# A two-number reordering in a hybrid-attention block: query norms two filler steps later, pair splits two attention steps later

## The chip, the cores and the metric

The kernel runs on one core of one Trainium2 chip. The metric is the device time of one execution in microseconds (us); lower is better. TensorE (PE in the profile) does the matrix products, and PEld is its weight load; VectorE is DVE, ScalarE is ACT, GpSimd is POOL; SP only starts transfers.

## The reference

One transformer block in float32, for 512 tokens of width 1024:

```
h = h + 0.5 * swiglu(rmsnorm(h, ffn1_norm), ffn1_w_gu, ffn1_w_down)
u = rmsnorm(h, mix_norm)
qa, ka, va, qb, kb, vb, qi, ki, wi, g = split(u @ w_in)
qa, ka, qb, kb = each head's rmsnorm, with its gain
out_a = dsa_attention(qa, ka, va, qi, ki, wi, bias_dsa)   # 8 heads, top-128 keys per query
out_b = moba_attention(qb, kb, vb, bias_moba)             # 8 heads, blocks of 256 keys
mixed = g_a * (out_a @ w_branch_dsa) + g_b * (out_b @ w_branch_moba)
h = h + mixed @ w_out
h = h + 0.5 * swiglu(rmsnorm(h, ffn2_norm), ffn2_w_gu, ffn2_w_down)
```

The heads are 64 wide, so two heads (a pair) fill 128 partitions. The hidden width of both feed-forward parts is 2816.

## The kernel before, in words

**Products.** Every float32 operand is split into a rounded high part and a low remainder, and each product is three matmuls (`mm3`, L126 to L128). A weight comes in by a transfer to `raw`, ACT writes `whi` (L111), POOL writes `wlo` in four pieces (L117). An activation is split by `split`: ACT writes the high part (L153), DVE the low one (L154).

**Stages.** First feed-forward part, then the mixer, then the second feed-forward part. The mixer runs the MoBA attention, the selection of keys, the MoBA branch, then the DSA attention and its branch. Each attention is a generator of 32 steps, for 8 heads times 4 tiles of 128 queries. Step `i` issues the logits of tile `i + 2` (PE L619 and L620 into one of two `s` banks; DVE L628 adds bias and takes the minimum; ACT L75 exponentiates), then `turn(i)` transposes the probabilities (PE L659, one to four 128-column transposes into a `pt` bank, which ACT L669 copies as the high part and DVE L670 as the low part), then, where `i % 4 == 1`, `values` of the head before: PE L680 and L681 into the one `o` bank, ACT L686, DVE L687 into `os`. After the second head of a pair POOL divides by the softmax sums (L690), and the pair's output is split (L153, L154). Its consumer, the branch product, runs only after all heads.

**What fills the gaps.** Between the steps `weave` takes units of the next projections as filler; every filler step is one `mm3` or a pair of them and calls `tick()`. Work that must not stand right behind its producer is queued with `later(n, fn)` and issued at the n-th tick from there. A query projection (`q_post`) squares its result (ACT L430 into a `tmp` buffer), and `later(LAG_Q, norm)` issues four tiny matmuls that sum the squares (L441, into a `pt` bank), DVE L444 that empties the bank, and a chain of small operations (ACT L75, DVE L447 to L451). A key projection does the like with `LAG` (L475, L476, L478, L479, L485, L486). Value projections end in ACT L500 and DVE L501, which empty an `mm` bank.

**Order and buffers.** The order on PE is the order in which the program is written; on the other engines a scheduler sets it. PSUM banks: `mm` 3, `s` 2, `pt` 2, `o` 1. A new `pt` tile takes whichever of the two banks comes free first, and its first matmul waits for the last reader of what the bank held.

Of the kernel before, what the change touches and what calls it, by code (L numbers as in the profile page):

```python
# [31 lines left out]

PIN, EVERY = (0, 20, 28, 31), 2

LAG, LAG_Q = 11, 4

SPIN, HURRY = 10, 200

# [7 lines left out]
def f32(ap):  # L46
    return ap.bitcast(F32)
# [3 lines left out]
def block_kernel(ctx, tc, x, gains, wgu1, wd1, w_in, w_v, wb_a, wb_b, w_out, wgu2, wd2, rel_bias, onehot, out):  # L51
# [30 lines left out]
    def log_exp(out, src, fn, **k):  # L82
        table_op("natural_log_exp_and_others", out, src, fn, **k)
# [3 lines left out]
    def T(tag, bufs, shape=(P, S), dt=F32, p=sb):  # L87
        uid[0] += 1
        return p.tile(list(shape), dt, tag=tag, name=f"{tag}{uid[0]}", bufs=bufs)

    def tmp(dt=F32):
        return T("tmp", TMPS, (P, S), dt)
# [4 lines left out]
    def sps():  # L97
        return T("s", 2, p=ps)

    def tps():  # L100
        return T("pt", 2, p=ps)
# [46 lines left out]
    def pair_a():  # L148
        return T("a", 16, (P, S), F32R), T("a", 16, (P, S), F32R)

    def split(dst, src):
        hi, lo = dst
        nc.scalar.activation(hi, src, AF.Copy)  # L153
        nc.vector.tensor_sub(lo, src, f32(hi))  # L154
        return dst
# [206 lines left out]
    def bias_tile(hd):  # L362
        t = T("bias", 2)
        f0 = fd[hd:hd + 1, 0:S]
        nc.sync.dma_start(t, bass.AP(f0.tensor, f0.offset, [[1, P], [1, S]]))
        return t
# [214 lines left out]
    def attention(br, pairs, outs, extra):  # L581

        sel = br == 0
        bias, prob, tms, osum, tot, inv_s = {}, {}, {}, {}, {}, {}

        def table(hd):
            if hd < 8:
                bias[hd] = bias_tile(br * 8 + hd)

        def rows(qt):  # L590
            return T(f"l{qt}", 2 if qt == 0 else 1, (P, P * (qt + 1)))

        def addend(i):

            if i < 32:
                hd, qt = divmod(i, 4)
                W = P * (qt + 1)
                inv = pairs[hd // 2][0][2][:, 2 * qt + hd % 2:2 * qt + hd % 2 + 1]
                tms[i] = rows(qt)
                b = bias[hd][:, S - W:S]  # L600
                if sel and qt:
                    nc.vector.scalar_tensor_tensor(tms[i], b, inv, work[:, WOFF[qt]:WOFF[qt] + W],
                                                   op0=ALU.mult, op1=ALU.add)
                else:
                    nc.gpsimd.tensor_scalar(tms[i], b, inv, 1.0, op0=ALU.mult, op1=ALU.mult)

        def logits(i):
            if i >= 32:
                return
            hd, qt = divmod(i, 4)  # L610
            if qt == 1:
                table(hd + 1)
            e = hd % 2
            (q, f, _), (k, kl), _ = pairs[hd // 2]
            W = P * (qt + 1)
            N = max(W, 256)
            p = sps()
            qb = q[:, e, qt * P:(qt + 1) * P]
            nc.tensor.matmul(p[:, 0:N], qb, k[:, e, 0:N], start=True, stop=False)  # L619
            nc.tensor.matmul(p[:, 0:N], qb, kl[:, e, 0:N], start=False, stop=True)  # L620
            addend(i + 1)
            pe = tms.pop(i)
            st = T("st", 8, (P, 4))
            if i % 8 == 0:
                tot[hd // 2] = T("tot", 2, (P, 8))
            s1 = tot[hd // 2][:, i % 8:i % 8 + 1]
            with tc.high_priority(HURRY):
                sums[i] = nc.vector.tensor_tensor_reduce(  # L628
                    out=pe, in0=p[:, 0:W], in1=pe, scale=f[:, 2 * qt + e:2 * qt + e + 1], scalar=3e38, op0=ALU.add, op1=ALU.min, accum_out=st[:, 0:1])
                log_exp(pe, pe, AF.Exp, bias=st[:, 0:1], scale=-1.0, accum_out=s1)  # L630
            prob[i] = pe

        def norms(pr, p):

            row = rows_d[turns[1] % 2]
            turns[1] += 1
            nc.vector.reciprocal(r1[:, 0:8], tot.pop(pr))
            nc.tensor.transpose(p, r1, ident)
            o = p[0:8, P - 1:P]
            rw = T("rw", 2, (8, P))  # L640
            nc.scalar.activation(rw, bass.AP(o.tensor, o.offset, [list(o.ap[0]), [-1, P]]), AF.Copy)
            nc.sync.dma_start(row, rw)
            rb = inv_s[pr] = T("rb", 2)
            for e in range(2):
                a = row[4 * e:4 * e + 1, :]
                nc.sync.dma_start(rb[HALF[e], :], bass.AP(a.tensor, a.offset, [[0, DH], [1, S]]))

        def turn(i):
            hd = i // 4
            if i % 4 == 0:  # L650
                return
            pp = tps()
            c, parts = 0, []
            for j in (i - 1, i) if i % 4 == 1 else (i,):
                qt = j % 4
                pe = prob.pop(j)
                parts.append((qt, pp[:, c:c + (qt + 1) * P].rearrange("p (k c) -> p k c", c=P)))
                for kt in range(qt + 1):
                    nc.tensor.transpose(pp[:, c:c + P], pe[:, kt * P:(kt + 1) * P], ident)  # L659
                    c += P  # L660
            if i % 8 == 6:
                norms(i // 8, pp[:, c:c + P])
            pth, ptl = pts[hd % 2]
            for qt, src in parts:
                def dst(a):
                    o = a[:, qt * P + P - 1:qt * P + P]
                    return bass.AP(o.tensor, o.offset, [list(o.ap[0]), [384, qt + 1], [-1, P]])

                nc.scalar.activation(dst(pth), src, AF.Copy)  # L669
                nc.vector.tensor_sub(dst(ptl), src, dst(f32(pth)))  # L670

        def values(hd):
            e = hd % 2
            v = pairs[hd // 2][2][0]
            pth, ptl = pts[hd % 2]
            po = T("o", 1, p=ps)
            for kt in range(NQ):
                q0 = min(kt, 2) * P
                c = 384 * kt + q0
                nc.tensor.matmul(po[:, q0:S], v[:, kt, e, :], pth[:, c:c + S - q0], start=kt == 0, stop=False)  # L680
                nc.tensor.matmul(po[:, q0:S], v[:, kt, e, :], ptl[:, c:c + S - q0], start=False, stop=kt == NQ - 1)  # L681
            if e == 0:
                osum[0] = T("os", 1)
            ot = tmp()
            with tc.high_priority(HURRY):
                nc.scalar.activation(ot[0:DH, :], po[DH:P, :], AF.Copy)  # L686
                nc.vector.tensor_add(osum[0][e * DH:(e + 1) * DH, :], po[0:DH, :], ot[0:DH, :])  # L687
            if e == 1:
                eng = nc.vector if sel and hd == 7 else nc.gpsimd
                eng.tensor_mul(osum[0], osum[0], inv_s.pop(hd // 2))  # L690
                outs.append(split(pair_a(), osum[0]))

        table(0)
        addend(0)
        logits(0)
        yield 2
        logits(1)
        yield 1
        for i in range(32):
            logits(i + 2)  # L700
            yield 1
            turn(i)
            yield 1
            if i % 4 == 1 and i > 4:
                values(i // 4 - 1)
            if extra and i % EVERY == 0:
                extra.pop(0)()
            yield 1
        yield 3
        values(7)  # L710

    def weave(att, filler, ahead):
        for _ in range(ahead):
            next(filler, None)
        for n in att:
            for _ in range(n):
                next(filler, None)
# [65 lines left out]
    for u, post in ((U_KI, ki_post), (U_QI, qi_post), (U_QI + 1, qi_post)):  # L783
# [5 lines left out]
    fill = chain(qk(1, 1) + qk(1, 2) + [vv(1, 1)] + qk(1, 3) + [gate(KD + c, gates) for c in range(GATES_B)]  # L789
                 + qk(0, 0) + [vv(0, 0)])  # L790
    weave(attention(1, moba, ob, extra), fill, AHEAD_B)
    run(fill)
    for qt in range(1, NQ):
        topk(qt)
    mixb = [T("a", 16) for _ in range(KD)]
    for c in range(KD):
# [3 lines left out]
        run(branch(wb_b, c, ob, lambda p: nc.vector.tensor_mul(mixb[c], p, g1)))  # L800
    fill = chain(qk(0, 1) + qk(0, 2) + [vv(0, 1)] + qk(0, 3) + [gate(c, gates) for c in range(GATES)])
    weave(attention(0, dsa, oa, []), fill, AHEAD_A)
    run(fill)
    flush()
# [105 lines left out]
```

## Time and profile before

| what | value |
|---|---|
| time of three runs | 1139.1, 1139.22, 1141.05 us (median 1139.22) |
| the profiled execution | 1139.47 us, span of its instructions 1137.7 us |
| granted TensorE clock | 1.000 over the whole span |
| busy: PE, DVE, ACT, POOL | 1130.0, 646.2, 469.9, 549.3 us |
| busy from 482 to 527 us: PE, DVE | 43.84, 43.71 of 45 us |

The profile is of one execution, 0.25 us above the median. The span leaves 1.77 us of it outside. Times in the rows are counted from the start of the span; "busy" of PE counts overlapping matmuls once. A name such as `pt` or `mm` stands for all tiles of that kind.

### The profile page before, as it was taken

To read this page: it belongs to the slowest core of one execution; us is meant where nothing else is said; L and a number is where in the kernel's file an instruction comes from. 1 tells how busy PE (TensorE), PEld (TensorE's weight loads), DVE (VectorE), ACT (ScalarE), POOL (GpSimd) and SP (SyncE) were. 2 spreads that over 40 slices of the span, in tenths; PEclk is the share of its full clock that TensorE was granted. 3 is DMA by queue.
4 is the path that set the end of the run, shared out by engine and by line. 5 is a ranking of instruction groups with operands and counts; after the bars stand their busy time and mean duration, and the time that the engine had idled before them with its cause. 6 is when DMAs were issued, how large, how long until landed. Compare 5 with 4: busy or idle time off the path is not lost.

```text
span 1137.7 us, 14242 instructions
## 1 busy us (share of the span) xinstructions
PE 1130.0 (99%) x5364; PEld 947.0 (83%) x5364; DVE 646.2 (57%) x971; ACT 469.9 (41%) x770; POOL 549.3 (48%) x435
## 2 busy tenths in 40 slices
PE   9999999999999999999999999999999999999998
PEld 8888888888888888888889888888888888888887
DVE  6853156613557458699958785754663156613641
ACT  6432123312325568768238766444332123212321
POOL 3444444444446574665564551174444444444443
PEclk9999999999999999999999999999999999999999
DMA  7233222322323222321232321422233232322322
GB/s 237 94 118 95 93 97 105 95 93 93 106 71 114 83 101 84 102 75 52 98 131 93 110 67 47 139 93 97 103 98 93 93 105 100 93 93 96 104 70 102
DMA packets 39580, 111.73 MB, mean 98 GB/s; under 512 B 4534, under 2 KB 9048, under 8 KB 39512
## 3 DMA queue, kind: packets, MB, share of 16 engines
q1 hardware_dynamic: 39080, 110.28, 29.4%
q8 instruction: 42, 0.69, 0.2%
q10 hardware_dynamic: 432, 0.55, 0.2%
q14 instruction: 26, 0.21, 0.1%
HBM read 108.64 MB, written 2.17 MB: 97 GB/s over the span
## 4 chain that ended last, share of the span: by engine, by line
PE 92%; DVE 5%; ACT 2%; issue 1%; POOL 1%; POOLq 0%; DVEq 0%
PE mm L126 22%; PE mm L127 22%; PE mm L128 22%; PE s L126 7%; PE s L128 7%; PE s L127 7%; PE pt L659 1%; DVE l L628 1%; PE s L619 1%; PE s L620 1%; DVE work L566 1%; PE o L681 1%; PE o L680 1%; POOL wlo L117 1%; DVE pt L670 0%
## 5 line engine op out<-in xcount | busy, mean ns | idle before, releaser
L117 POOL TENSOR_TENSOR wlo<-raw,whi 128x256 fp32r<-128x256 f32 (+2 forms) x344 | 491.6, 1449 | 528.7 <-ACT whi L111 517.4
L111 ACT ACTIVATE whi<-raw 128x1024 fp32r<-128x1024 f32 (+2 forms) x206 | 203.8, 994 | 509.5 <-PE mm L127 325.8
L126 PE MATMUL mm<-x,whi 128*128 128x512 f32 x630 | 249.6, 396 | 1.1 <-DVE v L501 1.1
L128 PE MATMUL mm<-x,wlo 128*128 128x512 f32 x630 | 245.9, 390 | 0.0
L127 PE MATMUL mm<-x,whi 128*128 128x512 f32 x630 | 245.9, 390 | 0.0
L126 PE MATMUL mm<-a,whi 128*128 128x512 f32 (+1 forms) x462 | 178.5, 386 | 0.0
L127 PE MATMUL mm<-a,whi 128*128 128x512 f32 (+1 forms) x462 | 178.5, 386 | 0.0
L128 PE MATMUL mm<-a,wlo 128*128 128x512 f32 (+1 forms) x462 | 178.4, 386 | 0.0
L128 PEld LDWEIGHTS mm<-x,wlo 128*128 128x128 f32 x630 | 118.2, 188 | 25.3
L126 PEld LDWEIGHTS mm<-x,whi 128*128 128x128 f32 x630 | 118.4, 188 | 22.8 <-DVE v L501 1.6
L127 PEld LDWEIGHTS mm<-x,whi 128*128 128x128 f32 x630 | 118.5, 188 | 21.3 <-DVE x L207 0.4
L126 PE MATMUL s<-x,whi 128*128 128x512 f32 x342 | 133.1, 389 | 0.0
L128 PE MATMUL s<-x,wlo 128*128 128x512 f32 x342 | 133.0, 389 | 0.0
L127 PE MATMUL s<-x,whi 128*128 128x512 f32 x342 | 133.0, 389 | 0.0
L289 DVE SCALAR_TENSOR_TENSOR h<-mm,h 128x512 f32<-128x512 f32 (+1 forms) x49 | 33.3, 681 | 167.6 <-PE mm L128 167.6
L275 DVE TENSOR_TENSOR tmp<-tmp,tmp 128x512 f32<-128x512 f32 x44 | 97.0, 2205 | 30.4 <-ACT tmp L75 30.1
L154 DVE TENSOR_TENSOR a<-tmp,a 128x512 fp32r<-128x512 f32 x49 | 86.4, 1764 | 28.5 <-ACT a L153 28.3
L126 PEld LDWEIGHTS mm<-a,whi 128*128 128x128 f32 x462 | 86.8, 188 | 17.6
L127 PEld LDWEIGHTS mm<-a,whi 128*128 128x128 f32 x462 | 86.8, 188 | 17.6
L128 PEld LDWEIGHTS mm<-a,wlo 128*128 128x128 f32 x462 | 86.8, 188 | 17.6
L128 PEld LDWEIGHTS s<-x,wlo 128*128 128x128 f32 x342 | 64.2, 188 | 13.4
L126 PEld LDWEIGHTS s<-x,whi 128*128 128x128 f32 x342 | 64.2, 188 | 13.3
(196 smaller groups left out, 1361.8 us busy)
## 6 DMA issues: line engine op xcount, KB each, us to landing
raw<-in_ffn_w_gu_dram SPq DMA_DIRECT2D x84, 512.0 KB, 3.5
raw<-in_w_in_dram SPq DMA_DIRECT2D x35, 512.0 KB, 3.5
raw<-in_ffn_w_down_dram SPq DMA_DIRECT2D x32, 512.0 KB, 3.5
raw<-in_ffn_w_down_dram SPq DMA_DIRECT2D x16, 384.0 KB, 3.1
bias<-fd SPq DMA_DIRECT2D x16, 256.0 KB, 3.4
raw<-in_w_v_dram SPq DMA_DIRECT2D x8, 512.0 KB, 3.4
raw<-in_w_out_dram SPq DMA_DIRECT2D x8, 512.0 KB, 3.5
raw<-in_ffn_w_gu_dram SPq DMA_DIRECT2D x16, 128.0 KB, 3.9
```

Of the source, the lines that this page charges most:

```text
L111: nc.scalar.activation(hi, raw, AF.Copy)
L117: eng.tensor_sub(lo[:, b], raw[:, b], f32(hi)[:, b])
L126: nc.tensor.matmul(pt, wh, xh, start=start, stop=False)
L127: nc.tensor.matmul(pt, wh, xl, start=False, stop=False)
L128: nc.tensor.matmul(pt, wl, xh, start=False, stop=stop)
L154: nc.vector.tensor_sub(lo, src, f32(hi))
L275: nc.vector.tensor_mul(g1, g1, s)
L289: nc.vector.scalar_tensor_tensor(h[c][:, b], pd, 0.5, h[c][:, b], op0=ALU.mult, op1=ALU.add)
L566: nc.vector.match_replace(out=acc, in_to_replace=m8, in_values=acc, imm_value=-2e38)
L619: nc.tensor.matmul(p[:, 0:N], qb, k[:, e, 0:N], start=True, stop=False)
L620: nc.tensor.matmul(p[:, 0:N], qb, kl[:, e, 0:N], start=False, stop=True)
L628: sums[i] = nc.vector.tensor_tensor_reduce(out=pe, in0=p[:, 0:W], in1=pe, scale=f[:, 2 * qt + e:2 * qt + e + 1], scalar=3e38, op0=ALU.add, ...
```

## The change

Two edits. `LAG_Q` goes from 4 to 6, so each query projection's four L441 matmuls, and with them the chain behind them, are issued two filler steps later; there are 8 such groups. And a finished pair's split (L153, L154) is no longer issued at the end of `values` but kept in a list, and `drop()` issues it at `i % 4 == 3`, two attention steps later; this holds for three pairs of each attention, while the last pair's is issued at once as before. Every instruction of before is there once; only places differ.

```diff
-LAG, LAG_Q = 11, 4
+LAG, LAG_Q = 11, 6
...
             if e == 1:
                 eng = nc.vector if sel and hd == 7 else nc.gpsimd
                 eng.tensor_mul(osum[0], osum[0], inv_s.pop(hd // 2))
-                outs.append(split(pair_a(), osum[0]))
+                done.append(osum[0])
+
+        done = []
+
+        def drop():
+            while done:
+                outs.append(split(pair_a(), done.pop()))
...
             if i % 4 == 1 and i > 4:
                 values(i // 4 - 1)
+            if i % 4 == 3:
+                drop()
             if extra and i % EVERY == 0:
                 extra.pop(0)()
             yield 1
         yield 3
         values(7)
+        drop()
```

How that moves instructions is shown at three places. The first is PE in the MoBA attention, from 425.7 to 428.5 us of the profile before: `pt_3255` (then `pt_3269`) holds the sums of squares, `pt_3283` the three transposes of a query tile. Before:

```order
L441 MATMUL pt_3255<-bd,tmp_3186 128x2 x4
L126 MATMUL mm_3193<-x_2536,whi_3195 128x512
L127 MATMUL mm_3193<-x_2537,whi_3195 128x512
L128 MATMUL mm_3193<-x_2536,wlo_3196 128x512
L619 MATMUL s_3272<-k_2959,q_2835 128x256
L620 MATMUL s_3272<-low_2642,q_2835 128x256
L126 MATMUL mm_3193<-x_2569,whi_3195 128x512
L127 MATMUL mm_3193<-x_2570,whi_3195 128x512
L128 MATMUL mm_3193<-x_2569,wlo_3196 128x512
L659 MATMUL pt_3283<-ident,l_3167 128x128 x3
```

And now:

```order
L126 MATMUL mm_3193<-x_2536,whi_3195 128x512
L127 MATMUL mm_3193<-x_2537,whi_3195 128x512
L128 MATMUL mm_3193<-x_2536,wlo_3196 128x512
L619 MATMUL s_3258<-k_2959,q_2835 128x256
L620 MATMUL s_3258<-low_2642,q_2835 128x256
L126 MATMUL mm_3193<-x_2569,whi_3195 128x512
L127 MATMUL mm_3193<-x_2570,whi_3195 128x512
L128 MATMUL mm_3193<-x_2569,wlo_3196 128x512
L441 MATMUL pt_3269<-bd,tmp_3186 128x2 x4
L659 MATMUL pt_3283<-ident,l_3167 128x128 x3
```

L441 went from eight matmuls ahead of the transposes to directly ahead of them. The same happens to the group of four L441 at 479.3 us and to that at 615.4 us, which in addition stood ahead of the eight L680 and L681 of `values` and now stands behind them.

The second place is DVE behind the group of 615.4 us, in the DSA attention, from 617.1 to 622.4 us: `pt_5452` is the pair of query tiles transposed before, whose second piece (128x2x128) L670 reads last, and `pt_5466` (then `pt_5500`) the sums of squares. Before:

```order
L444 TENSOR_TENSOR fq_5471<-pt_5466,r2q 128x8
L435 SCALAR_TENSOR_TENSOR q_5384<-mm_5309,gqk,q_5384 64x512
L670 TENSOR_TENSOR pt_2655<-pt_5452,pt_2654 128x128
L229 SCALAR_TENSOR_TENSOR tmp_5438<-mm_5434,tmp_5438 128x512
L687 TENSOR_TENSOR os_5489<-o_5480,tmp_5490 64x512
L628 ISA l_5423,st_5504<-s_5499,l_5423,fq_5264 128x128
L628 ISA st_5504 128x1
L478 SCALAR_TENSOR_TENSOR tmp_5438<-tmp_5438,tmp_5437 128x512
L670 TENSOR_TENSOR pt_2655<-pt_5452,pt_2654 128x2x128
```

And now:

```order
L435 SCALAR_TENSOR_TENSOR q_5384<-mm_5309,gqk,q_5384 64x512
L670 TENSOR_TENSOR pt_2655<-pt_5452,pt_2654 128x128
L229 SCALAR_TENSOR_TENSOR tmp_5438<-mm_5434,tmp_5438 128x512
L687 TENSOR_TENSOR os_5475<-o_5466,tmp_5476 64x512
L628 ISA l_5423,st_5490<-s_5485,l_5423,fq_5270 128x128
L628 ISA st_5490 128x1
L478 SCALAR_TENSOR_TENSOR tmp_5438<-tmp_5438,tmp_5437 128x512
L670 TENSOR_TENSOR pt_2655<-pt_5452,pt_2654 128x2x128
L479 TENSOR_TENSOR tmp_5437<-tmp_5301,tmp_5438 128x512
L444 TENSOR_TENSOR fq_5505<-pt_5500,r2q 128x8
```

L444 moved from eight rows ahead of the second L670 to two rows behind it; the rows between are the same.

The third place is ACT in the DSA attention from 633.7 to 638.2 us, where a pair's split met the value projection; the unsigned rows and the signs give the order before (-) and now (+):

```order
 L500 ACTIVATE v_5550<-mm_5407,r2T 128x2x64
-L153 ACTIVATE a_5653<-os_5489 128x512
+L669 ACTIVATE pt_2652<-pt_5685 128x3x128
 L500 ACTIVATE v_5550<-mm_5560,r2T 128x2x64
-L669 ACTIVATE pt_2652<-pt_5689 128x3x128
+L153 ACTIVATE a_5720<-os_5475 128x512
 L500 ACTIVATE v_5551<-mm_5407,r2T 128x2x64
```

L153 moved behind one L500 and one L669, but still stands ahead of the L500 that is the last to read `mm_5407` on ACT. On DVE its partner L154 moved from ahead of the L628 and L501 of this stretch to behind them.

## Rows read from the trace of the kernel before

**Rows 1.** The page: the span, PE's busy time, DVE and PEclk in 40 slices.

```profile
span 1137.7 us, 14242 instructions
...
PE 1130.0 (99%) x5364; PEld 947.0 (83%) x5364; DVE 646.2 (57%) x971; ACT 469.9 (41%) x770; POOL 549.3 (48%) x435
...
DVE  6853156613557458699958785754663156613641
...
PEclk9999999999999999999999999999999999999999
```

**Rows 2.** Timeline of PE, each late matmul and its predecessor: start, duration, what; [idle, releaser].

```profile
435.16 0.40 PE L127 MATMUL mm<-x,whi 128*128 128x512 f32 x1
435.39 0.39 PE L128 MATMUL mm<-x,wlo 128*128 128x512 f32 x1
436.53 0.50 PE L619 MATMUL s<-k,q 128*128 128x512 f32 x1 [0.75 <-DVE st L628]
...
522.60 0.28 PE L127 MATMUL mm<-wlo,x 128*128 128x256 f32 x1
522.72 0.28 PE L128 MATMUL mm<-whi,x 128*128 128x256 f32 x1
523.51 1.05 PE L441 MATMUL pt<-bd,tmp 128*128 128x2 f32 x8 [0.52 <-ACT tmp L430]
...
525.11 0.28 PE L128 MATMUL mm<-whi,x 128*128 128x256 f32 x1
526.03 0.66 PE L659 MATMUL pt<-ident,l 128*128 128x128 f32 x4 [0.64 <-DVE pt L670]
...
636.87 0.40 PE L128 MATMUL mm<-x,wlo 128*128 128x512 f32 x1
638.41 0.50 PE L126 MATMUL mm<-x,whi 128*128 128x512 f32 x1 [1.14 <-DVE v L501]
```

**Rows 3.** Timeline of PE and DVE around the first place, 426.6 to 430.2 us.

```profile
426.69 0.17 DVE L444 TENSOR_TENSOR fq<-pt,r2q 128x8 f32<-128x8 f32 x1 [0.94 <-PE pt L441]
...
428.22 0.49 PE L659 MATMUL pt<-ident,l 128*128 128x128 f32 x3
...
429.08 0.42 DVE L670 TENSOR_TENSOR pt<-pt,pt 128x256 fp32r<-128x256 f32 x1
```

**Rows 4.** Timeline of PE, DVE and POOL, 482.4 to 485.6 us.

```profile
483.09 0.49 PE L659 MATMUL pt<-ident,l 128*128 128x128 f32 x3
...
483.32 1.30 POOL L690 TENSOR_TENSOR os<-os,rb 128x512 f32<-128x512 f32 x1 [3.98 <-DVE os L687]
...
483.54 1.62 DVE L478 SCALAR_TENSOR_TENSOR tmp<-tmp,tmp 128x512 f32<-128x512 f32 x1
...
485.09 0.41 DVE L670 TENSOR_TENSOR pt<-pt,pt 128x256 fp32r<-128x256 f32 x1
```

**Rows 5.** Timeline of PE, ACT and DVE around the second place, 618.4 to 621.9 us.

```profile
619.21 0.49 PE L659 MATMUL pt<-ident,l 128*128 128x128 f32 x3
...
619.88 0.39 ACT L669 ACTIVATE pt<-pt 128x256 fp32r<-128x256 f32 x1
...
620.77 0.68 DVE L478 SCALAR_TENSOR_TENSOR tmp<-tmp,tmp 128x512 f32<-128x512 f32 x1
...
621.37 0.41 DVE L670 TENSOR_TENSOR pt<-pt,pt 128x256 fp32r<-128x256 f32 x1
```

**Rows 6.** Timeline of POOL, ACT and DVE around the third place, 633.6 to 638.5 us.

```profile
635.00 1.29 POOL L690 TENSOR_TENSOR os<-os,rb 128x512 f32<-128x512 f32 x1
...
636.33 0.63 ACT L153 ACTIVATE a<-os 128x512 fp32r<-128x512 f32 x1 [2.31 <-POOL os L690]
...
636.87 0.35 ACT L500 ACTIVATE v<-mm,r2T 128x128 fp32r<-128x128 f32 x1
636.99 0.69 DVE L154 TENSOR_TENSOR a<-os,a 128x512 fp32r<-128x512 f32 x1 [2.28 <-ACT a L153]
...
638.01 0.60 DVE L501 SCALAR_TENSOR_TENSOR v<-mm,r2T,v 128x128 fp32r<-128x128 f32 x2
```

## The prediction, as it was put on record

> **What bounds the kernel now.** I read the page first. PE is busy 99% of the span and the granted clock is 9 tenths or more in every slice [rows 1]; the reader is to see that PE sets the time, so that an edit matters only where it makes PE wait or takes a wait away. Then the list of waits and, at each place in it, the timeline of PE. One matmul of 512 columns starts 0.23 us after another (435.16 to 435.39), one of 256 columns 0.12 us (522.60 to 522.72) [rows 2]; whatever a start is later than that is a stall. In the two attentions I find four of any size: 436.53 − 435.39 − 0.23 = 0.91 us before the logits (an `s` bank that L628 empties), 523.51 − 522.72 − 0.12 = 0.67 us before L441, 526.03 − 525.11 − 0.12 = 0.80 us before L659, and 638.41 − 636.87 − 0.23 = 1.31 us before a key projection, whose bank L501 empties [rows 2]. Together 3.7 us: this is all that a reordering could take away here. Last I read the timelines of DVE, ACT and POOL around the places to which the change moves something, because the end of an operation there, against the nominal start on PE, tells whether PE would wait for it in the new order. DVE is at 9 tenths in the three slices from 483 to 569 us (slices 18 to 20) and has less to spare there than anywhere else in the attentions [rows 1].
>
> **The change part by part.** The counts are the same, so no busy time is added: the cost is in waits alone.
>
> *The L441 groups.* Four L441 take 0.8 us of PE wherever they stand, so the move by itself is free. What changes is the `pt` bank. There are two. In the old order L441 takes one bank eight or more matmuls ahead of the transposes; L444 empties it in 0.17 us, and the transposes take that same bank, long free: L444 ended at 426.86, the transposes started at 428.22 [rows 3]. In the new order L441 stands directly ahead of the transposes and holds the free bank, so that L659 must take the other one, and this is held until DVE's second L670 has read the previous tile. That is a new wait in the three places where the L659 follows at once.
>
> First place, MoBA's second pair: the second L670 ended at 429.08 + 0.42 = 429.50, L659 stands nominally at 428.22 in both orders [rows 3] (what moved behind the other matmuls is 0.8 us long and is put back in front of it). PE went on 0.05 us after such an end (526.03 against the 525.98 at which L670 ended), which gives 429.55 − 428.22 = 1.33. The two L75 and L444 of the query chain no longer precede it on ACT and DVE, and they took 0.1 to 0.2 us of that; I take 1.2, between 0.9 and 1.3.
>
> The stall of 0.91 at 436.53 comes after it. L628 reads logits made before the delay and its place on DVE changes little, so a PE that is 1.2 us late finds most of it gone: I take −0.76, between −0.91 and −0.3.
>
> Second, MoBA's fourth pair: nominal 483.09; the second L670 ended at 485.09 + 0.41 = 485.50 [rows 4], so 485.55 − 483.09 = 2.46. The reason for so late an end is the L478 ahead of it, which took 1.62 us, where the same operation took 0.68 in the DSA attention [rows 5]; POOL's L690 ran from 483.32 to 484.62 beside it [rows 4]. L690 starts when L687 ends, and that order is unchanged, so I keep 2.46; if L478 runs undisturbed the wait is 2.46 − 0.94 = 1.5, and that is the other end.
>
> The Trainium skill has a rule on this pair of operations (SBUF — State Buffer, Terms, "shared port pair"): DVE and GpSimd take one pair of ports exclusively for a whole instruction, and the one that comes later is blocked. The trace agrees in that L478 ended at 485.16, 0.54 us after L690 did. By that rule the 2.46 stays as long as L690 starts ahead of L478; without it, the 1.5 would be as likely.
>
> Next, 523 to 526 us: two stalls, 0.67 + 0.80 = 1.47, both because DVE is late [rows 1, 2]. PE arrives there later by what it lost at 428 to 483 (1.2 − 0.76 + 2.46 = 2.9), so both go. But in the new order the L441 group stands behind the L659 there, takes the bank that the second L670 of the tile before frees, and DVE has a further round of the key selection ahead of that. This gives back about 0.5; the change there is −1.0, between −1.47 (nothing comes back) and 0.
>
> Third, DSA's second pair: L659 nominally at 619.21; the chain ahead of the second L670 is ACT's L669 (619.88 to 620.27) and DVE's L687, L628 and L478 (to 621.45), and L670 ends at 621.37 + 0.41 = 621.78 [rows 5]. None of these moves in the new order, and none of them waits for PE. 621.83 − 619.21 = 2.62; I take 2.6, between 2.3 and 2.7. Here nothing stands behind that gives it back for 17 us.
>
> The other five groups have no L659 close behind, or one whose bank is free by more than they move; at some of these places the spare time is only a few tenths of a microsecond, so I put 0 there, up to +0.5 for all.
>
> *The splits.* Each is one L153 (0.63) and one L154 (0.69) [rows 6], and off PE's path but at one place, DSA's first pair: POOL's L690 ended at 636.29, L153 stood in front of two L500 on ACT until then, and L154 in front of L628 and of the L501 that freed the bank; PE went on 0.40 after the start of that L501 (638.01 to 638.41) [rows 6]. Now L154 is behind it, but L153 still stands ahead of the second L500. L153 starts at 636.33, the L500 behind it 0.54 later (636.87) as before, ends at 637.22, L501 starts there, PE goes on at 637.62. Nominal is 636.87 + 0.23 = 637.10, so 0.52 of the 1.31 stays: −0.8, between −1.31 (all of it) and 0 (L690 comes later). The other five splits move past work that no PE wait names; their consumers run after all heads, so I put 0.
>
> Sum: 1.2 − 0.76 + 2.46 − 1.0 + 2.6 − 0.8 = **+3.7 us** on the profiled execution's 1139.47, which is 1143.2. That execution is 0.25 above the median of the runs shown, so the forecast is 1143.0. Lower ends: 0.9 − 0.91 + 1.5 − 1.47 + 2.3 − 1.31 = +1.0, or 1140.2 by the median. Upper ends: 1.3 − 0.3 + 2.46 + 0 + 0.5 + 2.7 + 0 = +6.7, or 1145.9.
>
> **The rivals.**
>
> *Faster: the old stalls go and no new wait bites.* If DVE's second L670 comes early enough in all three places, only the gains are left: −0.91 (or 0, as no delay precedes it) − 1.31 and part of the 1.47, up to −3.7: 1135.5 to 1137. For it: the splits and the query chains really do move away from the L670 and L501. Against it: at 619.21 the L670 would have to end 2.6 us earlier, and no row ahead of it is removed [rows 5]. It decides only if all three new waits fall below 1 us in sum. Chance 0.06.
>
> *No change to be told.* All terms at their lower ends: 1140.2. For it: DVE may run L478 undisturbed, and PE's later arrival hides what is left at 523 to 526 us. A measurement of this kernel tells 0.2%, or 2.3 us, from no change, and +1.0 is inside that. Chance 0.24.
>
> *DVE is the bound from 482 to 527 us.* The operations that the selection of keys leaves no room for are then pushed behind the late PE as well, the stalls of 523 to 526 are as long as before, and the small margins elsewhere are used up: 1145.9. For it: the three 9s of DVE's row [rows 1]. Against it: DVE's own operations there need little from PE, so they run on while PE stands. Chance 0.13.
>
> *The clock falls.* The granted clock stayed at the upper of its two levels (2.4 GHz) through stalls of up to 1.31 us [rows 1, 2]; the new ones would be up to 2.6 us. If a stretch as long as the three waits together (6.3 us) then ran at half speed, matmuls that start 0.23 us apart would start 0.46 apart, and 3.1 us would come on top: 1146.1. No row shows the lower level. Chance 0.02. The Trainium skill describes such a case (TensorE: Matmul & The Clock Gate, "A second HAM failure mode: psum-queue depth-cycling"): a PE that idles often while it cycles through PSUM banks makes the clock swing between its levels. The trace of before has such idling without a swing, so I give it little.
>
> **How the numbers follow.** My forecast, a loss of 2.3 to 5.3 us, has 0.55, and its own range is 1141.5 to 1144.5. The predicted time is its centre, 1143.0. For 8 in 10 I add the DVE rival and most of the lower one: 1139.3 to 1146.0, which leaves out the faster case, the clock and a little at both ends. Slower by over 0.2% (above 1141.5) is 0.55 + 0.13 + 0.02 = 0.70, within 0.2% 0.24, faster 0.06.
>
> **What the profile of the changed kernel would show.** In PE's list of waits, L659 behind DVE's L670 with three new waits, of about 1.2, 2.4 and 2.6 us, the longest one second; the wait of the logits for L628 and that of L441 for ACT's L430 small or gone; the wait for L501 at about 0.5 in place of 1.31. PE's busy time unchanged, the span about 3.7 us longer, the clock 1.000. Each L441 group directly ahead of an L659 that starts after an L670 of 128x256 has ended. The prediction is wrong if L659 starts at once behind L441 in these places (then the bank was free, and I misread who holds it), if the wait for L501 stays above 1 us, or if another wait of over 1 us appears that I have not named.

## The result, and the profile after

The change makes the kernel slower: 1148.82 us (median of 4 runs, 1147.07 to 1150.25) against 1139.95 (4 runs, 1139.1 to 1141.05), a ratio of 1.0078 (95% interval 1.0065 to 1.0091), or 8.9 us. The forecast was 1143.0 with a range up to 1146.0. Direction and places were right; the size was not. The profiled execution took 1150.25 us, its span is 1148.5 (1137.7 before), and its mean granted clock is 0.996.

The page of after: the span, PE's busy time, and PEclk in 40 slices:

```profile
span 1148.5 us, 14253 instructions
...
PE 1134.8 (99%) x5364; PEld 952.2 (83%) x5364; DVE 648.0 (56%) x971; ACT 470.2 (41%) x770; POOL 546.2 (48%) x435
...
PEclk9999999999999999999999999999999999999999
```

Against [rows 1] hardly anything shows: PE is still 99% busy, and slices of 28.7 us are too coarse for what the clock did. The list of PE's waits, after (engine, line, operation, line waited for: us in total, times, longest):

```profile
PE pt L659 <- DVE pt L670: 6.9, 3, 3.2
PE pt L441 <- DVE pt L670: 1.1, 1, 1.1
PE o L175 <- DVE tmp L172: 1.1, 1, 1.1
PE mm L322 <- DVE whi L313: 1.0, 1, 1.0
PE pt L781 <- ACT tmp L778: 0.3, 1, 0.3
```

The three announced waits of L659 are there, and the stalls before the logits and before the key projection [rows 2] are gone. PE's timeline at the second and third wait, and at the one L441 that waits:

```profile
484.45 0.40 PE L128 MATMUL mm<-x,wlo 128*128 128x512 f32 x1
484.68 0.95 PE L441 MATMUL pt<-bd,tmp 128*128 128x2 f32 x8
488.08 0.87 PE L659 MATMUL pt<-ident,l 128*128 128x128 f32 x3 [2.45 <-DVE pt L670]
...
489.18 0.63 PE L127 MATMUL mm<-x,whi 128*128 128x512 f32 x1
489.61 0.63 PE L128 MATMUL mm<-x,wlo 128*128 128x512 f32 x1
...
530.98 0.28 PE L128 MATMUL mm<-whi,x 128*128 128x256 f32 x1
532.41 1.05 PE L441 MATMUL pt<-bd,tmp 128*128 128x2 f32 x8 [1.15 <-DVE pt L670]
...
624.50 0.95 PE L441 MATMUL pt<-bd,tmp 128*128 128x2 f32 x8
628.68 0.87 PE L659 MATMUL pt<-ident,l 128*128 128x128 f32 x3 [3.23 <-DVE pt L670]
...
630.42 0.41 PE L127 MATMUL mm<-wlo,x 128*128 128x256 f32 x1
630.63 0.41 PE L128 MATMUL mm<-whi,x 128*128 128x256 f32 x1
```

Read two things here. First the waits: an L441 group takes 0.8 us, so 488.08 − 484.68 − 0.80 = 2.60 us and 628.68 − 624.50 − 0.80 = 3.38 us of standing. Second the spacing behind them: matmuls of 512 columns start 0.43 us apart and those of 256 columns 0.21, where 0.23 and 0.12 are usual [rows 2]. The windows of these stretches give the clock (length, then busy time of PE, PEld, DVE, ACT and POOL with counts, then PEclk, DMA share, GB/s):

```profile
488.08:491.50 3.42, 3.42 (x10) 2.84 (x11) 2.43 (x5) 2.19 (x4) 0.58 (x1) 0.52 0.00 0
628.68:634.50 5.82, 5.82 (x28) 5.82 (x29) 3.14 (x7) 4.21 (x11) 0.00 (x0) 0.50 0.14 49
```

On DVE the second place is as it was [rows 4], L478 stretched again and L670 behind it:

```profile
486.02 1.59 DVE L478 SCALAR_TENSOR_TENSOR tmp<-tmp,tmp 128x512 f32<-128x512 f32 x1
487.53 0.41 DVE L670 TENSOR_TENSOR pt<-pt,pt 128x256 fp32r<-128x256 f32 x1
```

L670 ends at 487.94 and PE goes on at 488.08. For 3.4 us behind 488.08 and for about 6 us behind 628.68 (the window shows the first 5.8) the clock was at its lower level, 1.2 GHz, right after PE had stood for 2.6 and 3.4 us. In the third place it fell while PE still stood: over 627.70 to 628.60 the mean is 0.62 and no matmul runs. Behind the first of the three waits it stayed at 1.00 (426 to 436 us). PE counts as busy throughout, so neither its busy share nor the list of waits shows this. One number of the page does: PE's busy time grew from 1130.0 to 1134.8 us with the same 5364 matmuls.

The whole difference of 10.8 us between the two spans can be followed by how late each instruction of PE comes against before. "Nominal" stands for the L659 behind that L441, put right behind it, 0.8 us after the start of L441:

| up to | later than before, us | what was added |
|---|---|---|
| L781 at 386.73 (before: L772 at 384.57) | 2.16 | start of the kernel, nothing of the change |
| first L659 at 431.63 (428.22) | 3.41 | wait +1.25 |
| L441 at 484.68, nominal | 2.39 | wait of the logits gone, −1.02 |
| second L659 at 488.08 (483.09) | 4.99 | wait +2.60 |
| 491.58 (485.04) | 6.54 | lower clock +1.55 |
| L441 at 624.50, nominal | 6.09 | 523 to 526: two stalls out, one of 1.31 in, −0.45 |
| third L659 at 628.68 (619.21) | 9.47 | wait +3.38 |
| 634.54 (622.39) | 12.15 | lower clock +2.68 |
| the end | 10.8 | stall before the key projection gone, −1.3 |

The start differs between executions of kernels that are alike there: PE's first L322 waits 0.3 us in the profile of the run with `LAG_Q = 6` alone and 1.9 in that at five steps; in this profile the start costs 2.16. The change itself is 4.4 us of waits (old stalls that went are taken off) and 4.2 us of lower clock, 8.6 together, close to the 8.9 of the medians.

### The profile page after: what moved, and what is told of

Its sections match the earlier page's. It is cut to its first block, busy times and chain, and to the rows that moved or that the text cites. A ratio compares the mean times of both kernels' runs of the same rounds, so it can differ in the third digit from the quotient of the medians.

```text
span 1148.5 us, 14253 instructions
## 1 busy us (share of the span) xinstructions
PE 1134.8 (99%) x5364; PEld 952.2 (83%) x5364; DVE 648.0 (56%) x971; ACT 470.2 (41%) x770; POOL 546.2 (48%) x435
## 4 chain that ended last, share of the span: by engine, by line
PE 93%; DVE 3%; ACT 1%; issue 1%; DMA 0%; POOL 0%; SPq 0%; DVEq 0%; POOLq 0%
PE mm L126 22%; PE mm L127 22%; PE mm L128 22%; PE s L126 7%; PE s L127 7%; PE s L128 7%; PE pt L659 1%; PE s L619 1%; PE s L620 1%; PE o L681 1%; PE o L680 1%; DVE l L628 1%; DMA raw<-in_ffn_w_gu_dram 0%; PE pt L441 0%; DVE pt L670 0%
## 5 line engine op out<-in xcount | busy, mean ns | idle before, releaser
L154 DVE TENSOR_TENSOR a<-tmp,a 128x512 fp32r<-128x512 f32 x49 | 86.4, 1765 | 28.5 <-ACT a L153 28.3
L126 PEld LDWEIGHTS s<-x,whi 128*128 128x128 f32 x342 | 64.3, 188 | 13.4
L127 PEld LDWEIGHTS s<-x,whi 128*128 128x128 f32 x342 | 64.2, 188 | 13.3
```

What stands on the lines that cost most here:

```text
L126: nc.tensor.matmul(pt, wh, xh, start=start, stop=False)
L127: nc.tensor.matmul(pt, wh, xl, start=False, stop=False)
```

## The experiments

Each ratio is against executions of the kernel before that ran beside the experiment on the same chip. Their medians are 1140.65 us (each half alone, the bank, two groups filled), 1139.99 (five steps, and the runs on which groups matter) and 1140.09 (L444 ahead, all four filled, the selection). Line numbers shift by a few where lines were added: L660, L663 for L659, L671, L674 for L670.

**Each half alone.** `LAG_Q = 6` without the delayed split, and the delayed split with `LAG_Q = 4`:

```diff
-LAG, LAG_Q = 11, 4
+LAG, LAG_Q = 11, 6
```

> The query norms two filler steps later, the splits left where they were before. Theory (the L441 group that stands directly ahead of L659 takes the free pt bank): the same three waits of L659 for DVE's L670 as in the changed kernel (1.3, 2.5 and 2.6 to 3.4 us, list total about 6.9), the granted clock below 1.000 in the stretches behind the second and third, and 1147 to 1150 us. Rival (the moved splits, L153 and L154, hold up L670): at most a small loss, 1139 to 1142 us, clock 1.000.

> The splits two attention steps later, the query norms at 4 filler steps as before. Theory: no L659 waits for L670 by more than before (0.8 us), the wait for L501 near 638 us falls from 1.31 to about 0.5 us, clock 1.000, 1138.5 to 1140 us. Rival (the splits make the waits): L659 waits of over 1 us and 1145 us or more.

Measured: 1148.39 us (ratio 1.0066, 1.0054 to 1.0079), three waits of L659 for L670 with 7.1 us in the list, clock 0.994 to 0.997 in the five runs. The splits alone: 1139.31 us (0.999, 0.9982 to 0.9999), clock 1.000 in 9 of 11, no new wait, and the stall before the key projection near 638 us at 0.46 us in place of 1.31. So the whole loss is that of the query norms. The splits alone are worth about 1 us; on top of the late norms no gain is seen (1148.82 us with them, 1148.39 without).

**The bank.** The sums of squares in an `mm` bank instead of a `pt` bank:

```diff
-            pv = tps()[:, 0:2 * NQ]
+            pv = mmps()[:, 0:2 * NQ]
```

> The changed kernel, but the sums of squares take an mm bank (three of them) in place of a pt bank, so the L441 group still stands directly ahead of L659 and holds no pt bank. Theory (the bank, not the place in the order): none of the three waits, clock 1.000, 1136 to 1140 us, unless a projection now waits for an mm bank. Rival (the order itself, L441 behind values or ACT and DVE being late): the waits of L659 stay above 1 us, 1144 us or more.

Measured: 1146.42 us (1.0053, 1.0041 to 1.0066). The three waits of L659 are gone, as the theory said, but its time was missed, because others came:

```profile
PE mm L441 <- DVE q L435: 4.0, 4, 2.9
PE o L681 <- DVE pt L670: 2.5, 1, 2.5
```

L441 now waits for an `mm` bank that L435 empties, and PE comes to `values` at 441 us before L670 has written what L681 reads; the clock is 0.995 to 0.999. This run shows that the `pt` bank makes the three waits; it does not show what they cost.

**Five steps in place of six**, which puts L441 some matmuls ahead of L659:

```diff
-LAG, LAG_Q = 11, 6
+LAG, LAG_Q = 11, 5
```

> The changed kernel with all query norms at 5 filler steps: in the three places L441 stands five matmuls, not none, ahead of L659. Theory A (it is decided when the bank is given out: L444 comes behind L670 on DVE, so L659 takes the bank of L670): the three waits are as long as at 6 steps, the clock falls, 1146 to 1150 us. Theory B, as the prediction put it (L441 directly ahead of L659 is what does it): with 1 us between them the waits are gone or under 1 us, 1139 to 1142 us.

Measured: 1148.8 us (1.0066, 1.0048 to 1.0084), clock 0.993 to 0.999. Theory A holds. PE's timeline in the third place:

```profile
623.80 0.95 PE L441 MATMUL pt<-bd,tmp 128*128 128x2 f32 x8
...
625.52 0.28 PE L128 MATMUL mm<-whi,x 128*128 128x256 f32 x1
628.32 0.88 PE L659 MATMUL pt<-ident,l 128*128 128x128 f32 x3 [2.52 <-DVE pt L670]
```

And DVE's:

```profile
627.77 0.41 DVE L670 TENSOR_TENSOR pt<-pt,pt 128x256 fp32r<-128x256 f32 x1
628.10 0.67 DVE L479 TENSOR_TENSOR tmp<-tmp,tmp 128x512 f32<-128x512 f32 x1
628.70 0.15 DVE L444 TENSOR_TENSOR fq<-pt,r2q 128x8 f32<-128x8 f32 x1
```

Eight matmuls lie between L441 and L659 here, and still L659 waits for L670. The adjacency on PE, of which the prediction spoke, isn't what matters: L444 comes behind the second L670 on DVE, here and in the other two places, so that the other bank is the first to come free and L659 is given that one. Not all of this run's loss need be the three waits': in its profile the clock also fell in the start of the kernel (0.50 from 9.2 to 12.4 us, behind a wait of 1.9 us), which has nothing to do with the change.

**L444 ahead of L670 on DVE**, with L441 directly ahead of L659 as in the change:

```diff
-            nc.vector.tensor_mul(w, pv, r2q[:, 1])
+            with tc.high_priority(HURRY):
+                nc.vector.tensor_mul(w, pv, r2q[:, 1])
```

> The changed kernel with L444, which empties the bank of the sums of squares, at a higher priority, so that DVE runs it ahead of the second L670. L441 still stands directly ahead of L659. Theory (which of the two banks comes free first decides): L659 takes the bank of L441 and waits for L444 instead, some 0.3, 0.7 and 1.7 to 2.4 us in the three places in place of 1.3, 2.6 and 3.4, and the time falls to 1140 to 1144 us. Rival (the place of L441 in PE's order decides): as the changed kernel, 1147 to 1150 us.

Measured: 1142.26 us (1.0018, 1.0009 to 1.0026). DVE and PE in the third place:

```profile
621.66 0.15 DVE L445 TENSOR_TENSOR fq<-pt,r2q 128x8 f32<-128x8 f32 x1
...
622.33 0.41 DVE L671 TENSOR_TENSOR pt<-pt,pt 128x256 fp32r<-128x256 f32 x1
```

```profile
618.63 0.95 PE L441 MATMUL pt<-bd,tmp 128*128 128x2 f32 x8
621.87 0.55 PE L660 MATMUL pt<-ident,l 128*128 128x128 f32 x3 [2.29 <-DVE fq L445]
```

In the list, L659 waits for L444 (here L660 for L445) 3.1 us in three times, the longest 2.3, and no longer for L670. Beside the run before it this shows the cause from both sides: L441 apart from L659 and L444 late, all the loss; L441 next to L659 and L444 earlier, a quarter of it.

**Which groups.** A lag for each of the eight query norms, in order of issue:

```diff
-        later(LAG_Q, norm)
+        later(LAGS.pop(0), norm)
...
+    LAGS = [6, 4, 6, 4, 4, 6, 4, 6]
```

> The changed kernel, but the second, fourth, fifth and seventh query norm at 4 filler steps again; the first, third, sixth and eighth stay at 6. Theory (only the groups whose L659 then gets the bank of the tile before matter): no L659 waits over 1 us, clock 1.000, the time of the run with the splits alone, 1138.5 to 1140.5 us. Rival (the later chain behind L444 hurts in itself, wherever it stands): half of the loss or so is left, 1143 us or more.

> The changed kernel with only the seventh query norm at 6 filler steps, all others at 4. Theory (each such wait costs itself, and one of some 3 us a fall of the clock besides): L659 near 620 us waits 2.6 to 3.4 us for L670, the granted clock is near half speed for some 5 us behind it, the wait near 638 us is gone, together 1143 to 1145 us. Rival (the clock falls only because several long waits come in one execution): clock 1.000 and 1141.5 to 1142.5 us.

> The changed kernel with only the second query norm at 6 filler steps, all others at 4. Theory: L659 near 430 us waits about 1.3 us for L670 and takes the place of the 0.9 us that the logits waited near 437 us; too short for a fall of the clock, 1.000; 1139 to 1140.5 us. Rival (any wait for a bank brings the clock down): clock below 1.000 and 1141 us or more.

Measured: four groups late 1138.91 us (0.9988, 0.9979 to 0.9997), clock 1.000 in all 11 runs; the seventh alone 1143.04 (1.0022, 1.0012 to 1.0032); the second alone 1141.21 (1.0008, 0.9999 to 1.0016), above its 1139 to 1140.5 and, with a clock of 0.998 or 0.999 in 10 of 11 runs, inside the numbers of its rival. So the first, third, sixth and eighth group are harmless. The seventh alone gives the time that was expected, but in its profile not in the way that was expected (PE's windows; the eighth number is PEclk):

```profile
526.80:530.80 4.00, 4.00 (x21) 4.00 (x22) 3.90 (x10) 3.26 (x6) 0.00 (x0) 0.57 0.19 66
624.20:635.00 10.80, 10.80 (x86) 10.62 (x87) 8.47 (x23) 8.91 (x20) 2.22 (x3) 1.00 0.19 50
```

Behind its wait of 2.8 us (624.20) the clock stayed up; it fell behind the pair of old stalls near 524 and 527 us (0.51 and 0.80 us), where the kernel before has them too. Of its 12 runs, 2 show a clock of 1.000 and the others 0.996 to 0.999. The second group alone lost clock at the same pair, in its profile at 0.50 from 528 to 531 us; behind its wait of 1.2 us near 430 it stayed at 1.00, so the profile does not bear out the rival's reason. A single wait of up to 2.8 us therefore does not fix whether the clock falls; the same program does it in some executions and not in others. Over all profiles it is likely, though: ten waits for a bank or for L670 show 2.29 us or more in the brackets, and at eight of them the clock falls before the wait ends or within 1.4 us of its end (the two others are this one, 2.63 in brackets, and the 2.46 of L681 in the run with the `mm` bank).

**Filling the waits.** Matmuls whose result is overwritten, into the bank of the L441 groups, so that PE works where it would stand:

```diff
+            pv = tps()
+            for _ in range(FILL.pop(0)):
+                nc.tensor.matmul(pv, us[0][0][:, 0:P], us[0][0], start=True, stop=True)
+            pv = pv[:, 0:2 * NQ]
...
+    FILL = [0, 0, 0, 9, 0, 0, 12, 0]
```

> The changed kernel with 9 and 12 added matmuls of 512 columns into the bank of the fourth and the seventh L441 group (their result is overwritten), 2.1 and 2.8 us of PE work in the time in which PE otherwise stands. Theory (the clock falls because PE stands for 2.5 to 3.4 us): L659 starts as late as before, but the granted clock stays 1.000 and the stretches behind it run at full speed, which gives back about 5 us: 1143 to 1145 us. Rival (the clock falls for another reason, or its fall costs little): clock 0.996 to 0.997 and 1147 us or more.

> The changed kernel with added matmuls of 512 columns (0.23 us each, overwritten) in all four L441 groups behind which or before which PE stood over 1 us: 5, 11, 5 and 14. Theory (an execution loses clock only behind a stretch in which PE stands): the granted clock stays 1.000 in nearly every execution and the time is that of the waits alone, 1143 to 1145 us, so that the clock is worth 4 to 5 us of the changed kernel's loss. Rival (clock falls as often as with two groups filled): clock 0.997 to 0.999 in most executions and 1146 us or more.

Measured: two groups filled, 1146.44 us (1.0058, 1.0044 to 1.0071). The profiled run has clock 1.000 and 1144.89 us, inside the expectation; the other four have 0.997 to 0.999 and 1146.38 to 1147.7, so the expectation as a whole was missed: two of four waits are not enough. All four filled (5, 11, 5 and 14 matmuls in the second, fourth, fifth and seventh group), 1146.22 us (1.0054, 1.0042 to 1.0067), with clock 1.000, 1.000, 1.000, 0.999 and 0.999. The time was missed for a reason that the profile shows: in the fifth group the first added matmul itself waits for the bank,

```profile
PE pt L441 <- DVE pt L674: 1.2, 1, 1.2
```

so its five matmuls lie behind the wait and add 5 × 0.23 = 1.15 us. Without them it would be 1145.07. That is 5.0 us above before with the clock nearly at 1.000, and leaves 1148.82 − 1145.07 = 3.8 us of the change's loss for the clock. This is an estimate: the two medians were not measured side by side (before was at 1139.95 and 1140.09 beside them).

**A faster version.** The two old stalls of 523 to 526 us come from the key selection, which DVE runs in between. Starting its rounds later, on top of the four harmless late norms and the late splits:

```diff
-PIN, EVERY = (0, 20, 28, 31), 2
+PIN, EVERY = (0, 26, 31, 31), 2
```

> The run with four norms late and the splits late, and the key selection's rounds on DVE held back until the last step of the MoBA attention. Theory (the two waits near 525 us come from the selection's rounds ahead of L430's buffer and of L670 on DVE): both waits are gone, DSA's first logits are not late, 1137 to 1138.3 us, and fewer executions lose clock than in the kernel before. Rival (the selection then ends too late): a new wait of the logits for L628 near 600 us and 1139 us or more.

> As the run before it, with the selection held back only to step 26 of the MoBA attention, half as far. Theory: rounds still stand ahead of L670 near 525 us, so one of the two waits stays, 1138 to 1139 us. Rival: the same as with the full delay, 1137 to 1138 us.

Measured, half delay (26): 1137.77 us (0.9977, 0.9968 to 0.9986); full delay (31): 1138.25 (0.9985, 0.9976 to 0.9994). Both have clock 1.000 in all 11 runs, where 14 of the 27 runs of before beside them have less. The half delay was expected to be the slower of the two and is the faster, in the range of its rival: the full one brings waits of the logits at 492 and 598 us (0.78 and 0.45; the second is the wait that the rival named, without the rival's time), the half one leaves only 0.40 of the pair. What is left in the list of the half delay, in the attentions:

```profile
PE s L620 <- DVE st L629: 0.7, 1, 0.7
...
PE mm L126 <- DVE v L502: 0.3, 1, 0.3
...
PE pt L660 <- DVE pt L671: 0.2, 1, 0.2
```

It beats the kernel before by about 2.3 us and the change by 11. Some 1.1 us of the 2.3 is in the run with the four late norms already, which has the pair of stalls still.

## Why the prediction was wrong, point by point

**What bounds the kernel**: right. PE sets the time, and the loss is PE's waits and clock alone; its four old stalls were the places at which things happened.

**The L441 groups, where**: right. The three places are those of the prediction, and the fifth group's L441 waits as said. (The place that the prediction calls DSA's second pair is at the query projection of the third; its rows are the ones meant.) **Why**: right in the bank, wrong in what gives it out. The five-step run shows the waits without the adjacency, and the run with L444 ahead shows the adjacency without the wait for L670. The rule was on record ("whichever of the two banks comes free first"), but I did not apply it.

**Their sizes**: first place 1.25 for 1.2, second 2.60 for 2.46. The third is 3.38 for 2.6, outside the 2.3 to 2.7 that I gave. The step that failed for this term is "none of these moves in the new order": they do not, but what ran ahead of them did. DVE's L479 near 612 us, before and after (the POOL row is the four pieces of a weight's split):

```profile
605.50 0.69 DVE L479 TENSOR_TENSOR tmp<-tmp,tmp 128x512 f32<-128x512 f32 x1
605.51 3.86 POOL L117 TENSOR_TENSOR wlo<-raw,whi 128x256 fp32r<-128x256 f32 x4 [5.84 <-ACT whi L111]
```

```profile
611.78 1.18 DVE L479 TENSOR_TENSOR tmp<-tmp,tmp 128x512 f32<-128x512 f32 x1
611.67 3.28 POOL L117 TENSOR_TENSOR wlo<-raw,whi 128x256 fp32r<-128x256 f32 x4 [5.85 <-ACT whi L111]
...
628.13 0.41 DVE L670 TENSOR_TENSOR pt<-pt,pt 128x256 fp32r<-128x256 f32 x1
```

The delay is carried on: L479 ends 6.77 us later than before (606.19, 612.96) and the second L670 6.76 later (621.78 in [rows 5], 628.54), while PE is only 6.09 late. Before, DVE started 0.01 us ahead of POOL, took 0.69 us and POOL's four took 3.86; after, POOL was 0.11 ahead, DVE took 1.18 and POOL 3.28. The run with `LAG_Q = 6` alone is like the latter (1.18, third wait 3.38), the run with five steps and that with the seventh group alone like the former (0.69, third waits 2.68 and 2.78). In these five traces some 0.5 us of the third wait thus goes with which of two engines starts first. This is the rule of the Trainium skill that the prediction used for the second place (SBUF — State Buffer, Terms, "shared port pair": one instruction has the ports, the other is blocked); the five traces agree with it in which of the two is delayed, and I applied it to L478 alone.

**523 to 526 us**: −0.45 for −1.0. The wait of L441 there was 1.31, not 0.5, against the 1.47 of the two that went; the other 0.3 us are steps of about 0.1 us beside the stalls. The total lies inside the bounds that I gave.

**The splits**: the stall before the key projection is down by 0.85 in the run with the splits alone (0.8 forecast). In the changed kernel it is gone altogether, since PE comes later still.

**The sum of waits**: +4.4 for +3.7, well inside the bounds. The waits alone would have given some 1144 to 1145 us (1139.95 + 4.4, and 1145.07 with the waits filled), a time inside the range.

**The clock**: this is the step that failed and took the time out of the range. I gave it 0.02, because the clock "stayed at the upper of its two levels" in the trace of before, and 3.1 us. It fell behind two of the three waits in the profiled execution, and the mean clock is below 1.000 in all four runs; the rows give 4.2 us, the filled run 3.8. The mistake was the chance. One execution's trace does not speak for the others: of the 71 executions of before that ran beside the experiments, 33 show a clock of 0.999 and take some 1.5 us more, so the kernel lost clock now and then before the change, which the spread of three runs (1139.1, 1139.22, 1141.05) hinted at. The price was nearer: 3.1 us on top of the waits (1146.1) for the 4.2 that the rows show. With 4.2 in the sum the forecast would have been 1147.2; of the 1.6 us that are still missing, 0.7 are the waits (4.4 for 3.7) and 0.7 the median of before (1139.95 for 1139.22). PE's busy time, which I had called unchanged, is 4.8 us longer, mostly for the same reason. The section of the Trainium skill that I set aside (TensorE: Matmul & The Clock Gate, "A second HAM failure mode: psum-queue depth-cycling") describes a case near this one: a PE that is idle for short times, and often, while it cycles through PSUM banks, and a clock that swings. The trace agrees in the waits for a PSUM bank and in a clock that goes between 1.00 and 0.50; it differs in "often", since here two waits of 2.6 and 3.4 us were enough.

**What stays open**: what decides, in one execution, whether the clock falls. The length of one wait does not: it stayed up behind 2.8 us and fell behind 0.5 and 0.8 us in the same trace. Where the executions of before lose it was not traced; that the two programs in which the pair near 525 us is gone, or down to one stall of 0.40 us, kept 1.000 in 22 of 22 runs points to that pair, but the run with four late norms has the pair and kept it in 11 of 11.

## What to carry to other kernels

Moving an instruction that costs nothing can change which buffer its neighbour is given: with a pool of two PSUM banks, ask who reads a bank last and where that reader stands in its own engine's order, not how far apart the two writers stand. Where PE is the bound and runs without gaps, price a new wait twice, once for its length and once for a stretch at half speed that may follow it (here 3.4 to 6 us, at 1.6 and 2.7 us), and look at the clock of several executions, not of one. The gain lay elsewhere than the edit looked for it: in taking away short waits that were there before; in these runs every execution kept its clock, though the four late norms alone did the same.

## What the runs showed of the hardware that was not expected

The clock is at half speed for 3.4 us behind a wait of 2.6 us and for about 6 us behind one of 3.4 us in one execution, and stays up behind 2.8 us in another program's. Added matmuls in the waits kept it at 0.999 or 1.000 in all five runs, where the change alone had 0.996 to 0.997. And a DVE operation of 0.69 us becomes 1.18 when POOL starts 0.1 us ahead of it, while POOL's four pieces get 0.6 us shorter in turn.
